# Attention's matmuls in program order, and table products tied behind the softplus split

## The chip, the cores and the metric

The kernel runs on one core of a Trainium2 chip. The metric is device time in microseconds (us) of one execution; the kernel before takes 810.37 us, the median of three runs from 810.09 to 810.9 us.

## The reference, cut to what matters

One decoder layer on a sequence of 512 tokens of width 1024, in float32, with two token mixers side by side:

```
q, k, v, u, g_attn, g_ssm = split(x @ w_in)
A  = stick_breaking_attention(q, k, v) @ w_sb_out      # 8 heads of 64
     # z = q k / 8 ; w = exp(log_sigmoid(z) + sum over later keys of log_sigmoid(-z))
y  = s5_scan(u)                    # 32 groups of 16 channels, 64 complex states each
B  = glu(gelu(y) @ w_glu)
h  = LN1(alpha*x + (sigmoid(g_attn)*A + sigmoid(g_ssm)*B) @ w_o)
h  = LN2(alpha*h + convffn(h) + (p @ w_pe) * sigmoid(h @ w_pe_gate))
```

The S5 scan needs tables that depend on parameters alone (powers of a complex decay, their products with B and C); the kernel computes them on the chip, on DVE.

## The kernel before

Every operand of a matmul is split into a high and a low part (hi is a cast on ACT, lo a subtraction on DVE), and `mm3` makes three matmuls of a product: hi·hi, hi·lo, lo·hi. Weights arrive in pages of 128x1024 by DMA on SP's queue (L102); `split_to` casts them (ACT, L119, `wh`) and subtracts (DVE, L120, `wl`) one page ahead of use.

The stages are: projections u and v; the q/k projections of four pairs of heads; attention beside the projections of pairs 1 to 3 and beside the first of 16 gate projections; the S5 scan beside the other gates; then `mix_attn` (tile A), `mix_ssm` (tile mx), the output projection, the FFN. From the output projection on, nothing is touched by the change.

**Attention** works in 32 units, one for each head h and key block j (3, 2, 1, 0; widths of 128, 256, 384 and 512 queries). Stage a of a unit: three matmuls into z, then Exp and Ln on ACT (tile e), then on DVE a min/max (L210), a cast (L423) and a subtraction (L207) that split the softplus into `sp`. Stage b, five steps later: matmuls of `sp` with a triangle (`tri`) into the same z, two Exp on ACT (w and wp), a subtraction on DVE (wp's low part); the PSUM bank of z comes free here. Stage c, two steps after that: matmuls of wp with v into `av`. The tiles e and w rotate through a pool of six half pages, two or three of which are held by other tiles, so that the Exp of stage b writes to a half page that the softplus split of a recent unit must have left. There are eight PSUM banks for z, av and the projections.

**Order.** The Python program issues the work in an order that generators set: `feature_mms` yields after each third of a projection (8 contraction blocks as 3, 3, 2; called a quantum here), `advance` gives attention 6.5/6 steps for a quantum of q/k and 7/6 for a quantum of a gate, and `interleave` gives the S5 scan 4/3 steps for a quantum of the gates that are left. The S5 steps of a pair of groups pp are `ssm_in` (matmuls V), `ssm_rot`, `ssm_scan` (DVE) and `ssm_out` (matmuls y), with one step of lag from rot to scan and one from scan to out; after the last y a GELU, 16 small DMAs on SP (y<-yst, L828) and a split (yts) lead to the second half of mx. The first half of mx and all of A don't need them.

`Paced` hands out table work: at each step of attention `prep.give(PREP_A)` pays 0.8 us, and the generator `ssm_prep` issues instructions until its declared costs have used that up; what is left is issued after the last step.

The program order is not the order on the engines. The tile framework schedules the whole program by a simulated timeline: an instruction that is ready there may be put ahead of earlier ones on the same engine, and the order on each engine is then fixed. A dependency of the class NoSync between two instructions of one engine fixes their order and adds no semaphore; before, only `actf` uses it, to keep activation tables together.

Of the kernel before, what the change touches and what calls it, by code (L numbers as in the profile page):

```python
# [18 lines left out]
P = 128  # L19
# [150 lines left out]
class Layer:  # L170
# [21 lines left out]


    def mm(self, out, lhsT, rhs, start, stop):
        self.nc.tensor.matmul(out=out, lhsT=lhsT, rhs=rhs, start=start, stop=stop, skip_group_check=True)  # L195

    def mm3(self, out, ah, al, bh, bl, start, stop):
        self.mm(out, ah, bh, start, False)
# [5 lines left out]
        self.nc.vector.tensor_tensor(out=lo, in0=src, in1=hi.bitcast(F32), op=ALU.subtract)  # L204

    def tt(self, out, a, b, op):
        self.nc.vector.tensor_tensor(out=out, in0=a, in1=b, op=op)  # L207

    def stt(self, out, a, s, b, op0, op1):
        self.nc.vector.scalar_tensor_tensor(out=out, in0=a, scalar=s, in1=b, op0=op0, op1=op1)  # L210
# [4 lines left out]
    def actf(self, group, *args, **kw):  # L215

        ins = self.nc.scalar.activation(*args, **kw).ins  # L217
        if group != self.act_group:
            self.act_group, self.act_prev, self.act_cur = group, self.act_cur[-6:], []
        for p in self.act_prev:  # L220
            self.tc.add_manual_dep(ins, p.name, mybir.DependencyInfo(mybir.DependencyClass.NoSync,
                                                                     mybir.DependencyReason.DATA),
                                   reason="table order")
        self.act_cur.append(ins)


# [158 lines left out]
    def attention(self):  # L385

        nc = self.nc
        units = [(h, j) for h in range(NH) for j in (3, 2, 1, 0)]
        st = {}
        prep = self.prep  # L390

        def part(kind, h, j):

            key = (kind, h, j | 2 if j % 2 else j)
            if key not in st:
                st[key] = (self.halves.get(f"{kind}{h}_{j}", F32R, (P, 2, T // 2)) if j == 2 else
                           self.pages.get(f"{kind}{h}_{j}", F32R, (P, 2, T)))
            o = P if j == 1 else 0
            return st[key].t[:, :, o:o + T - P * j]

        def z_of(h, j):

            key = ("z", h, j | 2 if j % 2 else j)
            if key not in st:
                st[key] = self.banks.get(f"z{h}_{j}")
            o = P if j == 1 else 0
            return st[key].t[:, o:o + T - P * j]

        def stage_a(h, j):
            n, q0, r = T - P * j, P * j, slice(HD * (h % 2), HD * (h % 2) + HD)  # L410
            q1, q2, ks = self.qk[h // 2]
            z = z_of(h, j)
            self.mm(z, ks.t[:, h % 2, q0:q0 + P], q1.t[:, h % 2, q0:T], j != 1, False)
            self.mm(z, ks.t[:, h % 2, q0:q0 + P], q2.t[:, h % 2, q0:T], False, False)
            self.mm(z[:, 0:P], self.mask[:, 0], self.mask[:, 1], False, False)
            sp = part("sp", h, j)
            ep = self.halves.get(f"e{h}_{j}", F32, (P, T))
            e = ep.t[:, 0:n]
            self.actf(0, e, z, AF.Exp)
            self.actf(0, e, e, AF.Ln, bias=1.0)  # L420

            self.stt(e, e, 44.0, z, ALU.min, ALU.max)
            nc.vector.tensor_copy(sp[:, 0], e)  # L423
            self.tt(sp[:, 1], e, sp[:, 0].bitcast(F32), ALU.subtract)
            ep.free()

        def stage_b(h, j):
            n = T - P * j
            z, sp = z_of(h, j), part("sp", h, j)
            for half in range(2):  # L430
                self.mm(z, self.tri[:, 0], sp[:, half], False, False)
            for jj in range(j + 1, 4):
                spj = part("sp", h, jj)
                for half in range(2):
                    self.mm(z[:, P * (jj - j):n], self.tri[:, 1], spj[:, half], False, jj == 3 and half == 1)
            wp = part("wp", h, j)
            ep = self.halves.get(f"w{h}_{j}", F32, (P, T))
            w = ep.t[:, 0:n]
            self.actf(0, w, z, AF.Exp)
            self.actf(0, wp[:, 0], z, AF.Exp)  # L440
            if j != 3:
                st.pop(("z", h, j | 2 if j % 2 else j)).free()
            self.tt(wp[:, 1], w, wp[:, 0].bitcast(F32), ALU.subtract)
            ep.free()
            if j == 0:
                for key in (3, 2, 0):
                    st.pop(("sp", h, key)).free()

        def stage_c(h, j):

            q0 = P * j
            wp = part("wp", h, j)
            if j == 3:
                st["av", h] = self.banks.get(f"av{h}")
            av = st["av", h]
            vv = self.v[j].t[:, h].rearrange("p a d -> p (a d)")

            for half in range(2):
                self.mm(av.t[:, q0:T], vv, wp[:, half], j == 3 and half == 0, j == 0 and half == 1)
            if j != 3:  # L460
                st.pop(("wp", h, j | 2 if j % 2 else j)).free()
            if j == 0:
                if h % 4 == 0:
                    self.attn.append(self.pages.get(f"attn{h}", F32, (P, 2, T)))
                r, o = (slice(HD * x, HD * x + HD) for x in (h % 2, 1 - h % 2))
                out = self.attn[h // 4].t[r, (h // 2) % 2]
                nc.scalar.copy(out, av.t[o])
                self.tt(out, out, av.t[r], ALU.add)
                av.free()

        for s in range(len(units) + LAG_C):
            prep.give(PREP_A)
            if s == U_AT:
                self.ssm_u(0)
                self.ssm_u(1)
            if s < len(units):
                while units[s][0] // 2 not in self.qk:
                    yield False
                h, j = units[s]
                stage_a(h, j)  # L480
                if j == 0 and h % 2 == 1:
                    for pg in self.qk[h // 2]:
                        pg.free()
            if 0 <= s - LAG_B < len(units):
                stage_b(*units[s - LAG_B])
            if 0 <= s - LAG_C < len(units):
                stage_c(*units[s - LAG_C])
            yield True
        prep.give(math.inf)


# [156 lines left out]
    def cmul_wide(self, src, n, re, im):  # L648

        t1, t2 = (self.pages.get(f"cm{i}", F32, (P, 4, 16, 16)) for i in range(2))  # L650
        for t, v in ((t1, re), (t2, im)):
            self.tt(t.t[:, 0:n], src, v.unsqueeze(1).unsqueeze(3).to_broadcast([P, n, 16, 16]), ALU.mult)
            yield wide(256 * n)
        return t1, t2

    def ssm_prep(self):
# [2 lines left out]
        cb = self.cbp.t.rearrange("p c r k h -> p (c r) k h")  # L659

        t1, t2 = yield from self.cmul_wide(cb[:, 2:4], 2, *self.coef)
        self.tt(cb[:, 2], t1.t[:, 0], t2.t[:, 1], ALU.subtract)
        self.tt(cb[:, 3], t1.t[:, 1], t2.t[:, 0], ALU.add)
        t1.free()
        t2.free()
        for g in range(2):
            r, h = slice(64 * g, 64 * g + 64), slice(16 * g, 16 * g + 16)
            for ri, sign in ((0, 1.0), (1, -1.0)):
                nc.scalar.mul(self.b0.t[r, ri, :, h], cb[r, 2 + ri], sign)

        self.dd = self.cst.tile([32, 16, 32], F32, name="dd")
        self.tt(self.dd, self.ident[0:32, 0:32].unsqueeze(1).to_broadcast([32, 16, 32]),
                self.d32.unsqueeze(2).to_broadcast([32, 16, 32]), ALU.mult)
        yield wide(512) + 2 * wide(256)

        for m in range(1, 5):
# [3 lines left out]
            for dst, at, i in ((ca, m, 0), (ba, 4 - m, 2 - lo)):  # L680
                if dst is ca and m == 4:
                    continue
                for g in range(2):
                    r, h = slice(64 * g, 64 * g + 64), slice(16 * g, 16 * g + 16)
                    self.tt(dst[r, 0, :, at, h], t1.t[r, i], t2.t[r, i + 1], ALU.subtract)
                    self.tt(dst[r, 1, :, at, h], t1.t[r, i + 1], t2.t[r, i], ALU.add)
                    yield 2 * wide(256)
            t1.free()
            t2.free()
# [3 lines left out]
        for q in range(4):  # L693
            for ri in range(2):
# [2 lines left out]
                    nc.tensor.transpose(bank.t[:, k], ba[:, ri, 4 * q + k].rearrange("p j h -> p (j h)"), self.ident)  # L697
                nc.scalar.copy(self.bl[q].t[:, ri], bank.t)
                bank.free()
                yield wide(512)  # L700

        tab = self.tab = self.ssp.tile([P, 2, 16, P], F32, name="tab", tag="ba_tab")
        nc.vector.memset(tab[:, 0, :, 0:1], 1.0)
# [1 line left out]
        for i in range(7):  # L705
            m = 1 << i
            rot = self.rot[i]
            for k0, nk in ((0, 16),) if m < 64 else ((0, 8), (8, 8)):
# [2 lines left out]
                br, bi = (rot[:, c, ks].unsqueeze(1).unsqueeze(3).to_broadcast([P, 2, nk, m]) for c in range(2))  # L711
                old, new = tab[:, :, ks, 0:m], tab[:, :, ks, m:2 * m]
                n = nk * m
                self.tt(tp.t, old, bi, ALU.mult)
                yield wide(2 * n)
                self.tt(new, old, br, ALU.mult)
                yield wide(2 * n)
                self.tt(new[:, 0], new[:, 0], tp.t[:, 1], ALU.subtract)
                self.tt(new[:, 1], new[:, 1], tp.t[:, 0], ALU.add)
                tp.free()  # L720
                yield 2 * wide(n)

# [458 lines left out]

    def run(self):
        self.qk, self.attn, self.u4, self.pair = {}, [], {}, {}
        self.y, self.gate = [], []
        self.act_group, self.act_prev, self.act_cur = 0, [], []
        self.nc.scalar.preload_act_table_set("natural_log_exp_and_others")
# [11 lines left out]
            self.prep.give(PREP_QK)  # L1198
        att = self.attention()
        self.W.fa = 2  # L1200
        for pair in range(1, 4):
            advance(self.proj_qk(pair), att, QK_RATIO)
        gen = self.gates()
        advance(gen, att, G_RATIO, True)
        for pg in self.v:
            pg.free()
        interleave(gen, self.ssm(), SSM_RATIO)
# [12 lines left out]
        self.ffn_down()  # L1220


def advance(main, side, ratio, to_end=False):

    acc = 0.0
    for _ in main:
        acc += ratio
        while acc >= 1.0:
            acc -= 1.0
            r = next(side, None)  # L1230
            if r is None and to_end:
                return
            if r is False:
                acc = 0.0


@with_exitstack
# [99 lines left out]
```

## Time and profile before

| | us |
|---|---|
| median of 3 runs | 810.37 |
| the profiled execution, its own time | 808.88 |
| its span in the trace | 807.2 |
| PE busy (matmuls) | 789.1 (98%) |
| DVE busy | 509.9 (63%) |
| ACT busy | 331.5 (41%) |
| mean granted clock of PE, share of full | 0.991 |

Busy time of PE is the time in which a matmul is in flight; 18 us of the span have none. The clock that the chip grants to PE is a column of the views by stretches: 1.00 is 2.4 GHz, and a stretch at 1.2 GHz only would show 0.50. The profile is of one execution, and its own time is 1.49 us under the median of the runs.

### The profile page before, as it was taken

How to read it: one execution, taken by the hardware profiler on the slowest of the kernel's cores; microseconds unless marked ns; L12 is line 12 of the kernel's file. 1: busy time of each engine (PE TensorE's matmuls, PEld its weight loads, DVE VectorE, ACT ScalarE, POOL GpSimd, SP SyncE). 2: the span in 40 equal slices, each digit the busy share in tenths (PEclk: the TensorE clock that was granted, in tenths of full speed). 3: DMA queues.
4: the chain of work that ended last, by engine and by line, in shares of the span. 5: the costliest groups of instructions: out<-in, count | busy, mean ns of one | idle time of the engine just before them, and what ended most of it. 6: DMA issues, size and time to landing. Idle time of an engine off the chain costs nothing.

```text
span 807.2 us, 9738 instructions
## 1 busy us (share of the span) xinstructions
PE 789.1 (98%) x3716; PEld 660.2 (82%) x3716; DVE 509.9 (63%) x881; ACT 331.5 (41%) x538; POOL 24.4 (3%) x67
## 2 busy tenths in 40 slices
PE   9999889989999999999999999999999999999996
PEld 7888778878888878888888888888888888888885
DVE  6987975678876857847743756555565565422056
ACT  6435666654343544514433543433443444322000
POOL 0000000000000200004300000000000000000000
PEclk9999999989999999999999999999999999999999
DMA  9913221123113565424303232213312127421002
GB/s 319 390 53 88 70 72 33 53 79 112 45 53 105 208 210 172 166 79 152 109 27 122 85 107 75 84 51 105 105 63 94 53 78 261 157 105 52 1 27 78
DMA packets 29870, 86.73 MB, mean 107 GB/s; under 512 B 4224, under 2 KB 8448, under 8 KB 29568
## 3 DMA queue, kind: packets, MB, share of 16 engines
q1 hardware_dynamic: 27952, 80.35, 29.5%
q0 software_dynamic: 1296, 4.72, 1.6%
q10 hardware_dynamic: 576, 1.05, 0.3%
q8 instruction: 29, 0.48, 0.2%
q14 instruction: 17, 0.14, 0.0%
HBM read 79.81 MB, written 3.15 MB: 103 GB/s over the span
## 4 chain that ended last, share of the span: by engine, by line
PE 91%; DMA 3%; DVE 3%; ACT 2%; issue 1%; DVEq 0%; SPq 0%; ACTq 0%
PE up L195 30%; PE d L195 15%; PE g L195 10%; PE o L195 5%; PE pg L195 5%; PE mx L195 4%; PE z L195 3%; PE qb L195 3%; PE u L195 3%; PE kb L195 3%; PE v L195 3%; PE pe L195 1%; DMA y<-yst 1%; PE y L195 1%; PE av L195 1%; DMA wr<-in_w_sb_out_dram 1%
## 5 line engine op out<-in xcount | busy, mean ns | idle before, releaser
L120 DVE TENSOR_TENSOR wl<-wr,wh 128x1024 fp32r<-128x1024 f32 (+1 forms) x129 | 155.2, 1213 | 98.8 <-ACT wh L119 70.4
L195 PE MATMUL up<-hT,wh 128*128 128x512 f32 x704 | 216.6, 389 | 0.0
L119 ACT CAST wh<-wr 128x1024 fp32r<-128x1024 f32 (+1 forms) x129 | 133.5, 1044 | 161.2 <-PE d L195 38.1
L195 PEld LDWEIGHTS up<-hT,wh 128*128 128x128 f32 x704 | 132.1, 188 | 27.3
L195 PE MATMUL up<-hT,wl 128*128 128x512 f32 x352 | 136.9, 389 | 0.0
L195 PE MATMUL d<-wh,act 128*128 128x512 f32 (+1 forms) x364 | 109.1, 382 | 0.0
L210 DVE SCALAR_TENSOR_TENSOR cv<-up,cw,cv 128x511 f32<-128x511 f32 x88 | 65.8, 747 | 32.4 <-ACT cv L1120 30.9
L195 PE MATMUL g<-xs,wh 128*128 128x512 f32 x256 | 81.5, 398 | 0.0
L195 PEld LDWEIGHTS d<-wh,act 128*128 128x128 f32 x364 | 67.6, 188 | 13.2
L195 PEld LDWEIGHTS up<-hT,wl 128*128 128x128 f32 x352 | 66.1, 188 | 13.8
L195 PE MATMUL d<-wl,act 128*128 128x512 f32 (+1 forms) x182 | 69.5, 382 | 0.0
L1120 ACT ACTIVATE cv<-up,cb,cw 128x512 f32<-128x512 f32 x44 | 34.2, 777 | 59.0 <-PE up L195 59.0
L195 PEld LDWEIGHTS g<-xs,wh 128*128 128x128 f32 x256 | 46.5, 189 | 9.0 <-issue 0.6
L195 PE MATMUL g<-xs,wl 128*128 128x512 f32 x128 | 49.9, 391 | 0.0
L195 PE MATMUL pg<-wh,hT 128*128 128x512 f32 x128 | 40.1, 390 | 0.0
L195 PE MATMUL o<-wh,mx 128*128 128x512 f32 x128 | 40.1, 391 | 0.0
L195 PEld LDWEIGHTS d<-wl,act 128*128 128x128 f32 x182 | 34.2, 188 | 6.7
L195 PE MATMUL mx<-yts,wh 128*128 128x512 f32 x128 | 39.6, 389 | 0.0
L195 PE MATMUL z<-sp,tri 128*128 128x128 f32 (+3 forms) x160 | 30.5, 324 | 5.0 <-DVE e L210 2.1
L195 PEld LDWEIGHTS z<-sp,tri 128*128 128x128 f32 x160 | 27.4, 209 | 8.0 <-DVE sp L207 2.7
L207 DVE TENSOR_TENSOR cv<-cv 128x512 f32<-128x512 f32 x22 | 15.2, 692 | 24.5 <-ACT cv L217 24.5
L207 DVE TENSOR_TENSOR x<-x,d 128x512 f32<-128x512 f32 (+1 forms) x10 | 6.1, 606 | 35.1 <-PE d L195 35.1
(180 smaller groups left out, 1142.4 us busy)
## 6 DMA issues: line engine op xcount, KB each, us to landing
wr<-in_w_up_dram SPq DMA_DIRECT2D x44, 512.0 KB, 3.3
wr<-in_w_down_dram SPq DMA_DIRECT2D x22, 512.0 KB, 3.3
wr<-in_w_g_dram SPq DMA_DIRECT2D x16, 512.0 KB, 3.3
wr<-in_w_qk_dram SPq DMA_DIRECT2D x8, 512.0 KB, 11.7
wr<-in_w_glu_dram SPq DMA_DIRECT2D x8, 512.0 KB, 3.8
wr<-in_w_o_dram SPq DMA_DIRECT2D x8, 512.0 KB, 4.1
wr<-in_w_pe_gate_dram SPq DMA_DIRECT2D x8, 512.0 KB, 3.3
wr<-in_w_uv_dram SPq DMA_DIRECT2D x7, 512.0 KB, 7.6
```

The source lines that it names most:

```text
L119: self.nc.scalar.copy(hi.t[:, c], raw.t[:, c])
L120: self.nc.vector.tensor_tensor(out=lo.t[:, c], in0=raw.t[:, c], in1=hi.t[:, c].bitcast(F32), op=ALU.subtract)
L195: self.nc.tensor.matmul(out=out, lhsT=lhsT, rhs=rhs, start=start, stop=stop, skip_group_check=True)
L207: self.nc.vector.tensor_tensor(out=out, in0=a, in1=b, op=op)
L210: self.nc.vector.scalar_tensor_tensor(out=out, in0=a, scalar=s, in1=b, op0=op0, op1=op1)
L1120: nc.scalar.activation(y, bank.t, AF.Identity, scale=cw[:, 2:3], bias=cb)
```

## The change

The matmuls from the projection of pair 1 to the end of attention are chained in program order by NoSync dependencies. Each wide table product and sum on DVE is chained behind the last softplus split issued before it. `advance` starts the first of its calls with minus one step, so attention's first unit is issued one quantum later. The seven last steps of attention, which have no stage a, count as 1.8 steps, so more gate quanta are issued beside them. The declared cost of a transposition of the table `ba` falls from wide(512), 0.69, to 0.3, so that more table work is issued for the same pay. No instruction is added or removed.

```diff
     def mm(self, out, lhsT, rhs, start, stop):
-        self.nc.tensor.matmul(out=out, lhsT=lhsT, rhs=rhs, start=start, stop=stop, skip_group_check=True)
+        ins = self.nc.tensor.matmul(out=out, lhsT=lhsT, rhs=rhs, start=start, stop=stop, skip_group_check=True).ins
+        if self.in_order:
+            if self.last_mm is not None:
+                self.after(ins, self.last_mm)
+            self.last_mm = ins
+
+    def after(self, ins, prev):
+        self.tc.add_manual_dep(ins, prev.name, mybir.DependencyInfo(mybir.DependencyClass.NoSync,
+                                                                    mybir.DependencyReason.DATA), reason="order")
+    def tt_wide(self, out, a, b, op):
+        ins = self.tt(out, a, b, op)
+        if self.last_sp is not None:
+            self.after(ins, self.last_sp)
...
-            self.tt(sp[:, 1], e, sp[:, 0].bitcast(F32), ALU.subtract)
+            self.last_sp = self.tt(sp[:, 1], e, sp[:, 0].bitcast(F32), ALU.subtract)
...
                 while units[s][0] // 2 not in self.qk:
-                    yield False
+                    yield 0.0
...
-            yield True
+            yield 1.0 if s < len(units) else 1.8
...
-            self.tt(t.t[:, 0:n], src, v.unsqueeze(1).unsqueeze(3).to_broadcast([P, n, 16, 16]), ALU.mult)
+            self.tt_wide(t.t[:, 0:n], src, v.unsqueeze(1).unsqueeze(3).to_broadcast([P, n, 16, 16]), ALU.mult)
...
                 nc.scalar.copy(self.bl[q].t[:, ri], bank.t)
                 bank.free()
-                yield wide(512)
+                yield 0.3
...
         self.W.fa = 2
+        self.in_order = True
         for pair in range(1, 4):
-            advance(self.proj_qk(pair), att, QK_RATIO)
+            advance(self.proj_qk(pair), att, QK_RATIO, start=-1.0 if pair == 1 else 0.0)
         gen = self.gates()
         advance(gen, att, G_RATIO, True)
+        self.in_order = False
...
-def advance(main, side, ratio, to_end=False):
-    acc = 0.0
+def advance(main, side, ratio, to_end=False, start=0.0):
+    acc = start
     for _ in main:
         acc += ratio
         while acc >= 1.0:
-            acc -= 1.0
             r = next(side, None)
             if r is None and to_end:
                 return
-            if r is False:
-                acc = 0.0
+            acc = acc - (r or 1.0) if r != 0.0 else 0.0
```

The other calls of `self.tt` in `cmul_wide` and `ssm_prep` (tiles cm, cb, dd, ca, ba, tabtmp, tab) become `self.tt_wide` in the same way.

## Rows read from the trace of the kernel before

**Rows 1.** Busy time by engine in stretches from attention to the end of A

```profile
core 0: us, PE busy (x) PEld busy (x) DVE busy (x) ACT busy (x) POOL busy (x), PEclk, DMA share, GB/s
64.00:124.00 60.00, 54.40 (x286) 46.89 (x285) 50.07 (x103) 36.04 (x82) 0.00 (x0) 0.97 0.25 74
124.00:176.00 52.00, 49.28 (x267) 42.89 (x267) 32.13 (x79) 34.86 (x77) 0.00 (x0) 0.93 0.19 61
...
199.00:279.00 80.00, 80.00 (x454) 68.67 (x453) 63.01 (x105) 33.84 (x61) 2.02 (x10) 1.00 0.31 98
279.00:304.00 25.00, 24.40 (x108) 19.86 (x107) 13.10 (x18) 13.57 (x15) 2.95 (x6) 1.00 0.63 218
```

**Rows 2.** The same view, the stretches of 4 us around the two largest stalls

```profile
116.00:120.00 4.00, 1.82 (x10) 1.16 (x8) 3.89 (x11) 1.60 (x3) 0.00 (x0) 1.00 0.38 87
120.00:124.00 4.00, 3.27 (x11) 2.98 (x12) 3.91 (x9) 2.29 (x6) 0.00 (x0) 0.58 0.20 46
164.00:168.00 4.00, 1.67 (x12) 1.38 (x10) 3.90 (x16) 2.69 (x7) 0.00 (x0) 1.00 0.41 133
168.00:172.00 4.00, 3.64 (x12) 2.95 (x13) 2.88 (x7) 2.58 (x6) 0.00 (x0) 0.56 0.67 200
172.00:176.00 4.00, 4.00 (x18) 3.61 (x18) 2.61 (x7) 3.62 (x9) 0.00 (x0) 0.59 0.21 60
```

**Rows 3.** Waits from 64 to 199 us: total, times, longest in us

```profile
ACT w L217 <- DVE sp L207: 15.8, 9, 4.4
...
PE z L195 <- DVE e L210: 2.7, 2, 2.1
...
PE z L195 <- DVE sp L207: 2.0, 1, 2.0
...
PE qb L195 <- ACT wp L217: 1.1, 1, 1.1
```

**Rows 4.** Timeline of DVE at the first large stall: start, us, instruction

```profile
118.06 1.18 DVE L207 TENSOR_TENSOR ba<-cm,cm 64x256 f32<-64x256 f32 x3
...
119.53 0.42 DVE L207 TENSOR_TENSOR ba<-cm,cm 64x256 f32<-64x256 f32 x1
119.98 0.69 DVE L207 TENSOR_TENSOR sp<-e,sp 128x512 fp32r<-128x512 f32 x1
```

**Rows 5.** Timeline of PE behind that split, idle time before it in brackets

```profile
120.73 2.18 PE L195 MATMUL z<-sp,tri 128*128 128x512 f32 x7 [2.04 <-DVE sp L207]
```

**Rows 6.** Timeline of DVE before attention's first unit

```profile
56.77 1.53 DVE L207 TENSOR_TENSOR ca<-cm,cm 64x256 f32<-64x256 f32 x4
58.31 1.53 DVE L207 TENSOR_TENSOR ba<-cm,cm 64x256 f32<-64x256 f32 x4
```

**Rows 7.** Chain of waits: the projection behind q of pair 0

```profile
60.43 5.44 PE kb L195 x24
```

**Rows 8.** Timeline of SP: the DMAs of q, pair 0

```profile
61.08 2.53 SPq L380 DMA_DIRECT2D q<-q  x4
```

**Rows 9.** View of tile q from 50 to 75 us: issue to landing

```profile
DMA to landing us min/median/max: 2.2/2.3/3.1
```

**Rows 10.** Matmuls grouped by line, 199 to 271 us: the gates

```profile
L195 PE MATMUL g<-xs,wh 128*128 128x512 f32 x144 | 46.0, 401 | 0.0
L195 PE MATMUL g<-xs,wl 128*128 128x512 f32 x72 | 28.1, 390 | 0.0
```

**Rows 11.** Timeline of PE: last V, and mx's second half

```profile
261.80 1.05 PE L195 MATMUL V<-u,bl 128*128 128x128 f32 x8
...
270.86 0.62 PE L195 MATMUL A<-ats,wh 128*128 128x512 f32 x2
...
303.05 0.84 PE L195 MATMUL mx<-yts,wh 128*128 128x512 f32 x3
```

**Rows 12.** DVE grouped by line, 262.8 to 276.5 us: what is not the scan

```profile
L120 DVE TENSOR_TENSOR wl<-wr,wh 128x1024 fp32r<-128x1024 f32 x3 | 3.7, 1218 | 0.2 <-ACT wh L119 0.2
L207 DVE TENSOR_TENSOR yts<-y,yts 128x512 fp32r<-128x512 f32 x2 | 2.2, 1090 | 0.0
```

More of the change, by code (lines that the diff above doesn't have):

```diff
@@ L206, in tt @@
     def tt(self, out, a, b, op):
-        self.nc.vector.tensor_tensor(out=out, in0=a, in1=b, op=op)
+        return self.nc.vector.tensor_tensor(out=out, in0=a, in1=b, op=op).ins
+    def tt_wide(self, out, a, b, op):
+        ins = self.tt(out, a, b, op)
+        if self.last_sp is not None:
+            self.after(ins, self.last_sp)
     def stt(self, out, a, s, b, op0, op1):
@@ L220, in actf @@
         for p in self.act_prev:
-            self.tc.add_manual_dep(ins, p.name, mybir.DependencyInfo(mybir.DependencyClass.NoSync,
-                                                                     mybir.DependencyReason.DATA),
-                                   reason="table order")
+            self.after(ins, p)
         self.act_cur.append(ins)
@@ L661, in ssm_prep @@
         t1, t2 = yield from self.cmul_wide(cb[:, 2:4], 2, *self.coef)
-        self.tt(cb[:, 2], t1.t[:, 0], t2.t[:, 1], ALU.subtract)
-        self.tt(cb[:, 3], t1.t[:, 1], t2.t[:, 0], ALU.add)
+        self.tt_wide(cb[:, 2], t1.t[:, 0], t2.t[:, 1], ALU.subtract)
+        self.tt_wide(cb[:, 3], t1.t[:, 1], t2.t[:, 0], ALU.add)
         t1.free()
@@ L671, in ssm_prep @@
         self.dd = self.cst.tile([32, 16, 32], F32, name="dd")
-        self.tt(self.dd, self.ident[0:32, 0:32].unsqueeze(1).to_broadcast([32, 16, 32]),
+        self.tt_wide(self.dd, self.ident[0:32, 0:32].unsqueeze(1).to_broadcast([32, 16, 32]),
                 self.d32.unsqueeze(2).to_broadcast([32, 16, 32]), ALU.mult)
@@ L684, in ssm_prep @@
                     r, h = slice(64 * g, 64 * g + 64), slice(16 * g, 16 * g + 16)
-                    self.tt(dst[r, 0, :, at, h], t1.t[r, i], t2.t[r, i + 1], ALU.subtract)
-                    self.tt(dst[r, 1, :, at, h], t1.t[r, i + 1], t2.t[r, i], ALU.add)
+                    self.tt_wide(dst[r, 0, :, at, h], t1.t[r, i], t2.t[r, i + 1], ALU.subtract)
+                    self.tt_wide(dst[r, 1, :, at, h], t1.t[r, i + 1], t2.t[r, i], ALU.add)
                     yield 2 * wide(256)
@@ L713, in ssm_prep @@
                 n = nk * m
-                self.tt(tp.t, old, bi, ALU.mult)
+                self.tt_wide(tp.t, old, bi, ALU.mult)
                 yield wide(2 * n)
-                self.tt(new, old, br, ALU.mult)
+                self.tt_wide(new, old, br, ALU.mult)
                 yield wide(2 * n)
-                self.tt(new[:, 0], new[:, 0], tp.t[:, 1], ALU.subtract)
-                self.tt(new[:, 1], new[:, 1], tp.t[:, 0], ALU.add)
+                self.tt_wide(new[:, 0], new[:, 0], tp.t[:, 1], ALU.subtract)
+                self.tt_wide(new[:, 1], new[:, 1], tp.t[:, 0], ALU.add)
                 tp.free()
@@ L1183, in run @@
         self.qk, self.attn, self.u4, self.pair = {}, [], {}, {}
+        self.in_order, self.last_mm, self.last_sp = False, None, None
         self.y, self.gate = [], []
```

## The prediction, made before the change was run

> **What bounds the kernel now.** I read the busy times by stretches first, to see where PE, which is busy for 98% of the span, is not. In the scan's stage, between 199 and 279 us, PE has no idle time at all [rows 1]; a change of order can win nothing there and can only lose. Attention is the place: PE is idle for 60.00 - 54.40 = 5.60 us between 64 and 124 us and for 52.00 - 49.28 = 2.72 us between 124 and 176 us, 8.32 us together [rows 1]. Then I cut these stretches into pieces of 4 us, to see what follows an idle time. Behind the two largest ones (2.18 us of 116 to 120, 2.33 us of 164 to 168) the mean granted clock falls to 0.58, 0.56 and 0.59, a mix of the 2.4 and the 1.2 GHz level; at these means the three pieces lose 4 x (0.42 + 0.44 + 0.41) = 5.1 us of matmul time [rows 2]. So attention's stalls cost at most 8.3 + 5.1 = 13.4 us. "At most", since idle time inside a slow piece is counted twice.
>
> What ends the stalls is in the waits: of PE's own, 4.7 us are for DVE's min/max and softplus split, and the largest wait of all is ACT's, 15.8 us for the split, because the Exp of stage b writes to a half page that the split must have left [rows 3]. DVE is not idle then: in both pieces with a stall it is busy for 3.89 and 3.90 of 4 us [rows 2]. The timeline shows with what. Four sums of the table ba stand directly ahead of the subtraction of a split [rows 4], and PE, which has its triangle matmuls next, stands still for 2.04 us [rows 5]. The scheduler put those matmuls there for a simulated DVE that was earlier than the real one.
>
> **The change, part by part.** Nothing is added to any engine: no matmul, product or DMA more, and the chains are between instructions of one engine, so no semaphore. All terms are order.
>
> *The table tie* takes the cause of the large stalls away: a product may not pass the split issued before it. It is a wait for DVE too: a tied product whose split is late holds up the weight splits (wl) and wp subtractions queued behind it, for which the gates and av wait. It forbids what the kernel does now at 56.77 us, where eight table sums, 1.53 + 1.53 us, fill DVE before the first unit exists [rows 6]; by the pay, three of the four pairs of sums belong to attention's first steps, 2.3 us that move into the fullest stretch. There DVE was busy for 50.07 us [rows 1]; with 2.3 more it needs 52.4 us, and PE without its stalls would want 60 - 5.6 - 1.7 = 52.7 us. At the 3.9 of 4 us that DVE reaches at its fullest [rows 2], 52.4 us of work take 53.7 us. So DVE gives back 1 us if its waits are hidden, and all 5.6 us of idle time there if it does no better than the 83% of before; I take 2 us, nearer to its fullest pieces, since they show that it can.
>
> *The matmul chain.* In program order stage b follows stage a by five steps, with 6 quanta beside 6.5 units. A quantum is a third of 5.44 us [rows 7], so five steps hold some 8 us of projections and the units' own matmuls, against a softplus chain of five instructions, none longer than the widest subtraction's 0.69 us [rows 4], so at most 3.5 us if nothing is ahead of them (an estimate). That margin is what the scheduler's order spent. The price is that whatever is late holds the whole queue. Writing the order down by hand, I count 12 places where a PSUM bank is asked for 1.4 to 2.8 us of matmuls after the work that frees it (two Exp on ACT, or the copy of av). Today such a wait costs PE 1.1 us, once [rows 3]. The bounds are 0 and 12 x 1.1 = 13 us; I take 3 us, a quarter of a microsecond each, because ACT is busy for only 36 of 60 us there [rows 1] and most of these distances are above 2 us.
>
> *The first unit* comes after two quanta instead of one. q ends at 60.43 us, where the next projection begins [rows 7]; its four DMAs are issued in 2.53 us from 61.08 us on [rows 8], and land 2.2 to 3.1 us later [rows 9]. The first two, which unit 0 needs, land at about 64.1 us. Two quanta of 3/8 x 5.44 = 2.04 us each put its matmuls at 64.5 us. No stall; one quantum earlier it would be 62.5 us, and 1.6 us lost under the chain. Cost nothing, with 0.4 us of cover; uncovered, at most the 3.1 - 2.2 = 0.9 us by which a landing varies [rows 9].
>
> *More gates beside the last units.* With 5 + 6 + 6 units beside q/k instead of 18, and seven last steps at 1.8, attention takes 15 + 12.6 = 27.6 credits and ends in the 25th gate quantum; before, 21 credits and the 19th. So 23 quanta, not 29, are left beside the scan. On the chip the difference is smaller: the trace has 216 gate matmuls from 199 us on, 27 quanta [rows 10], so two had been pulled forward. Their weight DMAs move along on SP, past the loads of u; at a DMA share of 0.19 to 0.25 [rows 1] I charge nothing, and if that cover went, a page's landing would show as PE waiting for wl. PE's work is the same in sum. What it uncovers is the end of the scan. Of the scan's 36 steps 30 are now issued beside gates, so the last V comes behind the last gate. Now V starts at 261.80 us and the second half of mx, which needs the y after it, at 303.05 us [rows 11]: 41.2 us that PE fills, but for 0.60 us idle [rows 1], with y, A, the first half of mx, and, between V and A's start at 270.86 us [rows 11], 6.8 us of gates (30 matmuls at 5.44/24). If V goes behind the gates, those 6.8 us are missing. The hole is 0 if the scheduler pulls V forward as it does now, or if DVE drops other work from the way: three wl and two yts, 3.7 + 2.2 us [rows 12], stand between V and y. I take 2.5 us: those splits belong to A and mx and only some can go elsewhere.
>
> *The cheaper transpositions* issue table work earlier: 8 x 0.39 = 3.1 us of pay, four steps. It uses DVE's idle time of 124 to 176 us (52 - 32.13 = 19.9 us [rows 1]). Nothing, unless the gates beside it lose their wl.
>
> **Sum.** -13.4 + 2 + 3 + 2.5 = -5.9 us. On the profiled execution, 808.88 us, that is 803.0 us; the median of the runs stands 1.49 us above it, so I forecast 804.5 us.
>
> **Rivals.** *All of it.* DVE keeps up, ACT frees the banks in time, V is pulled forward; only 1 us stays: -12.4 us, 798.0 us. For it speaks that each stall of more than 2 us has table work in it; against it, that DVE needs 99% of the q/k stretch. Chance 0.15.
>
> *The buffers, not the order.* If all 12 bank places cost the 1.1 us that one costs now, 13.2 us come back and the time is 810.2 us, no change. For it: the 15.8 us of ACT are a wait for a half page [rows 3]. Against it: the table sums in the middle of a split are an order, and they are untied from no buffer. Chance 0.12. The Trainium skill, Perfetto Trace Analysis, Optimization Strategy, says that the same gap repeating on the engine that should be saturated can mean that SBUF or PSUM lacks room for the next tile; by that rule order would change little here. The trace agrees for ACT's wait and not for PE's two long stalls, which are of different lengths, 48 us apart.
>
> *Slower: the end of the scan.* The hole takes its full 6.8 us, and a hole of that kind is followed by a slow clock as in attention (up to 4 x (0.44 + 0.41) = 3.4 us [rows 2]): 10.2 us against a gain of 13.4 - 2 - 3 = 8.4 us, +1.8 us, 812.2 us. It decides where the hole exceeds what attention wins, and with DVE at its other bound (5.6 for 2) it is +5.4 us. For it: PE is full there and mx waits for 16 DMAs that nothing shortens. Against it: A can start earlier, and the scheduler is not chained in that stage. Chance 0.17. That the chain changes nothing is excluded: the trace has triangle matmuls ahead of older work.
>
> **How the numbers follow.** The forecast has 0.56, the rivals 0.15, 0.12 and 0.17. About 0.2%, 1.6 us, is what a measurement of this kernel can tell from no change. Faster holds the forecast less 0.01 and the first rival, 0.70; same 0.13; slower 0.17. The range runs from just under the first rival, 797.5 us, to the slower one, 812.5 us; beyond it lie DVE's worst bound with a full hole and a gain without any remainder. The forecast's own range is 800 to 808.5 us.
>
> **What would show it.** Right: between 64 and 176 us of work PE idles for 2 to 6 us, the clock stays at 1.00, no table product stands inside a split, and ACT's wait for sp falls well under 15.8 us; gates from 199 us on fall to about 23 quanta; the stall before mx's second half grows to some 3 us. Wrong: many PE waits of about 1 us for wp or attn (the buffers), a wait of 5 us or more for yts or a slow clock near 280 us (the scan's end), or DVE over 97% busy with PE waiting for sp throughout.

## The result, and the profile after

The changed kernel takes 802.47 us, the median of five runs from 802.31 to 803.08 us, against 810.9 us for the kernel before beside it: a ratio of 0.990, with a 95% interval from 0.9885 to 0.9914. The profiled execution is the run of 802.31 us, with a span of 800.6 us; it stands 0.16 us under its median. The forecast was 804.5 us.

The busy times by stretch, as in [rows 1] (PE, PEld, DVE, ACT, POOL, granted clock, DMA share, GB/s):

```profile
64.00:124.00 60.00, 58.10 (x308) 49.34 (x307) 54.99 (x116) 39.99 (x88) 0.00 (x0) 1.00 0.28 82
124.00:176.00 52.00, 48.47 (x277) 42.05 (x277) 39.73 (x91) 34.22 (x75) 0.00 (x0) 1.00 0.16 52
...
199.00:271.00 72.00, 72.00 (x410) 61.39 (x410) 52.94 (x92) 30.07 (x55) 0.74 (x7) 1.00 0.27 88
271.00:300.00 29.00, 27.63 (x133) 22.79 (x133) 20.02 (x29) 15.56 (x17) 3.95 (x8) 1.00 0.60 200
```

PE's idle time in attention fell less than one might think, from 5.60 + 2.72 = 8.32 us to 1.90 + 3.53 = 5.43 us, and in the second stretch it even rose. The clock column is what changed wholly: 0.97 and 0.93 became 1.00 and 1.00. The same view in the pieces of 4 us that hold the three largest stalls answers to [rows 2]:

```profile
108.00:112.00 4.00, 3.18 (x19) 2.71 (x18) 3.91 (x9) 2.81 (x7) 0.00 (x0) 1.00 0.00 0
136.00:140.00 4.00, 2.51 (x17) 2.15 (x17) 2.74 (x6) 3.97 (x9) 0.00 (x0) 1.00 0.00 0
164.00:168.00 4.00, 2.37 (x14) 1.81 (x13) 3.94 (x9) 1.96 (x5) 0.00 (x0) 1.00 0.00 0
```

The pieces lack 0.82, 1.49 and 1.63 us of PE, where before they lacked 2.18 and 2.33 us, and no piece from 60 to 200 us is below 1.00 in the clock. So the chip kept 2.4 GHz throughout attention. The waits of 64 to 199 us, as in [rows 3]:

```profile
ACT w L232 <- DVE sp L216: 4.5, 4, 1.5
...
PE z L195 <- ACT wp L232: 2.0, 3, 1.6
...
PE bt L710 <- ACT wp L232: 1.0, 1, 1.0
PE av L195 <- ACT wp L232: 0.8, 1, 0.8
...
PE z L195 <- DVE e L225: 0.6, 1, 0.6
PE z L195 <- DVE attn L216: 0.6, 1, 0.6
...
PE av L195 <- DVE attn L216: 0.3, 1, 0.3
```

ACT's wait for the half page that a split must leave went from 15.8 to 4.5 us, and PE no longer waits for a split (sp) at all. Of what is left, 3.8 us are for the Exp that frees a PSUM bank or fills wp, and 1.5 us for DVE's min/max (e) and its sum of attention's outputs (attn).

At the end of the scan, PE's timeline, which answers to [rows 11]:

```profile
261.09 1.06 PE L195 MATMUL V<-u,bl 128*128 128x128 f32 x8
261.90 0.71 PE L195 MATMUL A<-ats,wh 128*128 128x512 f32 x2
...
297.08 1.66 PE L195 MATMUL mx<-yts,wh 128*128 128x512 f32 x6 [1.37 <-DVE yts L903]
```

The last V stands behind the last gate now, with A directly after it, and the second half of mx waits 1.37 us; before, 0.60 us of the same stretch was idle. And the gates from 199 us on, as in [rows 10]:

```profile
L195 PE MATMUL g<-xs,wh 128*128 128x512 f32 x118 | 37.9, 402 | 0.0
L195 PE MATMUL g<-xs,wl 128*128 128x512 f32 x60 | 23.4, 390 | 0.0
```

That is 178 matmuls or 22 quanta, against 27.

The account of the profiled executions: idle time of attention -2.9 us, slow clock -5.1 us, the end of the scan +0.8 us, -7.2 us in all, where their own times differ by 802.31 - 808.88 = -6.6 us. So attention gave back 8.0 us.

### The profile page after: what moved, and what is told of

It is laid out like the page before. It is cut to its first block, busy times and chain, and to the rows that moved or that the text cites. A ratio compares the mean times of both kernels' runs of the same rounds, so it can differ in the third digit from the quotient of the medians.

```text
span 800.6 us, 9760 instructions
## 1 busy us (share of the span) xinstructions
PE 784.6 (98%) x3716; PEld 655.8 (82%) x3716; DVE 508.2 (63%) x881; ACT 333.1 (42%) x538; POOL 24.2 (3%) x67
## 4 chain that ended last, share of the span: by engine, by line
PE 92%; DVE 3%; ACT 2%; DMA 2%; issue 1%; SPq 1%; DVEq 0%; ACTq 0%
PE up L195 30%; PE d L195 15%; PE g L195 10%; PE o L195 5%; PE pg L195 5%; PE mx L195 4%; PE z L195 3%; PE u L195 3%; PE v L195 3%; PE kb L195 2%; PE qb L195 2%; PE A L195 2%; PE pe L195 1%; PE y L195 1%; DMA y<-yst 1%; PE av L195 1%
## 5 line engine op out<-in xcount | busy, mean ns | idle before, releaser
L195 PEld LDWEIGHTS mx<-yts,wh 128*128 128x128 f32 x128 | 24.0, 188 | 6.7 <-DVE yts L903 1.8
L195 PEld LDWEIGHTS g<-xs,wl 128*128 128x128 f32 x128 | 24.0, 188 | 5.2
```

Source lines behind the costliest of these rows:

```text
L195: ins = self.nc.tensor.matmul(out=out, lhsT=lhsT, rhs=rhs, start=start, stop=stop, skip_group_check=True).ins
```

## The experiments

All runs below are of five rounds beside the kernel before, whose medians were 810.28, 810.18 and 810.57 us in the three groups, and 810.9 us beside the changed kernel; times are medians. Between groups the same kernel thus moved by 0.7 us, so a difference of less than 1 us between groups is not shown by the times alone. The diffs of the first six (down to 36/23 scan steps in the table) are against the changed kernel. For each I also read two numbers from its trace, both from 60 to 200 us: PE's idle time, and the clock loss, the sum over pieces of 4 us of 4 x (1 - mean granted clock). They are of the one profiled execution. A piece without a matmul counts too, so that 1.2 us of the 5.1 us of "no tie" cost no matmul time.

| kernel | us | PE idle, 60 to 200 | clock loss |
|---|---|---|---|
| before | 810.2 to 810.9 | 8.3 | 5.1 |
| changed | 802.47 | 5.4 | 0.0 |
| changed, no chain | 804.5 | 2.6 | 3.4 |
| changed, no tie | 814.32 | 14.0 | 5.1 |
| changed, first unit early | 803.99 | 4.7 | 0.0 |
| changed, tail at 1.0 | 801.7 | 5.4 | 0.0 |
| changed, old pay | 801.73 | 3.9 | 0.0 |
| changed, 36/23 scan steps | 801.47 | 5.4 | 0.0 |
| chain alone | 810.85 | 11.0 | 5.1 |
| tie alone | 809.98 | 7.9 | 6.9 |
| tie and tail | 812.52 | 7.9 | 6.9 |
| tie and first unit | 802.58 | 4.7 | 5.1 |
| chain and tie | 801.28 | 5.1 | 0.0 |
| chain, tie and first unit | 799.73 | 3.8 | 0.0 |

Three of these executions lose clock once more, outside the columns: "no chain", "first unit early" and "tie and tail" lose some 1.7 us each behind PE's wait for yts near 300 us.

**One part taken back: the chain.**

```diff
-        self.in_order = True
+        self.in_order = False
```

> The changed kernel without the matmul chain (in_order stays False); tie, first unit, tail of 1.8 and cheap transpositions stay. Theory 'the chain': the scheduler's own order of matmuls is what stands PE still, so most of the 8.4 us go back: 808 to 812 us, with stalls of 2 us and more in attention and a granted clock under 0.95 behind them. Rival 'the table tie': the products inside the split were the cause, the chain adds nothing: 801 to 804 us, clock 1.00.

804.5 us, from 802.41 to 806.40 us in two groups of three; ratio to before 0.9926 (0.9905 to 0.9948). So the chain is worth some 2 us in this company, and not most of the gain. That it is worth anything here is not clear of noise: the intervals of the two ratios overlap (from 0.9905 here, up to 0.9914 for the changed kernel), and three of the six runs, up to 802.94 us, are as quick as the changed kernel's. The profiled run, of 806.4 us, has less idle time in attention than the changed kernel, but a stall that the clock follows. Busy times of three pieces:

```profile
104.00:108.00 4.00, 2.33 (x9) 1.79 (x8) 3.94 (x8) 2.24 (x5) 0.00 (x0) 0.72 0.21 79
108.00:112.00 4.00, 3.73 (x11) 2.98 (x11) 3.91 (x9) 3.52 (x7) 0.00 (x0) 0.50 0.00 0
112.00:116.00 4.00, 4.00 (x20) 3.44 (x20) 3.96 (x10) 0.52 (x3) 0.00 (x0) 0.93 0.00 0
...
300.00:304.00 4.00, 4.00 (x12) 3.08 (x12) 4.00 (x6) 1.05 (x1) 0.00 (x0) 0.57 0.13 52
```

PE lacks 1.67 us in the first piece, after which a whole piece runs at 0.50: 1.2 GHz. But attention is the smaller part of it: its span is 4.1 us longer than the changed kernel's (804.7 for 800.6 us), and attention makes 0.6 us of that, 2.8 us less idle time against 3.4 us of slow clock. The rest stands at the start, where PE waits 1.6 us for the first split of x, and at the end of the scan, where it waits 2.00 us for yts instead of 1.37 and the clock then falls, as the last line shows (4 x 0.43 = 1.7 us).

**The tie.**

```diff
         ins = self.tt(out, a, b, op)
-        if self.last_sp is not None:
-            self.after(ins, self.last_sp)
```

> The changed kernel without the tie of the wide table products; the chain stays. Theory 'the chain': little is lost, 802 to 805 us, PE idle in attention of 5 to 8 us in pieces under 2 us. Rival 'the table tie': 807 to 811 us, since products again run ahead of the splits and the chained PE waits for them.

814.32 us, 4 us over the kernel before (ratio 1.005, 1.0033 to 1.0068): more than either expected, 11.9 us for the one part. The timelines of three engines show the whole mechanism in one place. DVE first:

```profile
171.37 0.35 DVE L434 CAST sp<-e 128x384 fp32r<-128x384 f32 x1
171.75 0.42 DVE L223 SCALAR_TENSOR_TENSOR e<-e,z 128x256 f32<-128x256 f32 x1
172.09 2.35 DVE L216 TENSOR_TENSOR tab<-tab,pair_buf 128x1024 f32<-128x1024 f32 x2
174.36 0.55 DVE L216 TENSOR_TENSOR sp<-e,sp 128x384 fp32r<-128x384 f32 x1
174.83 0.29 DVE L434 CAST sp<-e 128x256 fp32r<-128x256 f32 x1
175.15 0.42 DVE L216 TENSOR_TENSOR sp<-e,sp 128x256 fp32r<-128x256 f32 x1
```

Two products of the table, 2.35 us, sit between the cast and the subtraction of a split (128x384). The next split (128x256), whose min/max is done before them, comes behind both. ACT wants the half page of this second split for w:

```profile
175.61 0.38 ACT L230 ACTIVATE w<-z 128x256 f32<-128x256 f32 x1 [6.01 <-DVE sp L216]
```

And PE, which wants the PSUM bank that this Exp and the one after it free, and, being chained, does nothing else meanwhile:

```profile
176.32 1.22 PE L195 MATMUL z<-q,ks 128*128 128x512 f32 x2 [7.63 <-ACT wp L230]
```

**The first unit.**

```diff
-            advance(self.proj_qk(pair), att, QK_RATIO, start=-1.0 if pair == 1 else 0.0)
+            advance(self.proj_qk(pair), att, QK_RATIO, start=0.0)
```

> The changed kernel with the first unit one quantum earlier (start 0). By the timing of q's DMAs (landing at about 64.1 us, matmuls wanted at 62.5 us) the chained PE waits 1.6 us at the first unit: 803.5 to 805 us, with one idle piece near 62 to 64 us. Rival: the wait is made up later, since attention as a whole has slack at its tail: 802 to 803 us.

803.99 us, from 803.14 to 804.34, so 1.5 us slower. PE's waits show the wait for q that the expectation put at 1.6 us, and a longer one at the end of the scan:

```profile
PE mx L195 <- DVE yts L903: 2.2, 1, 2.2
...
PE z L195 <- DMA q<-q: 1.4, 2, 1.0
```

The wait for q isn't where the time went, though. In attention as a whole PE idles less than in the changed kernel, 4.7 us for 5.4, so the early wait is made up within attention, as the rival expected. What is longer is the wait for yts, 2.16 us for 1.37, and the clock falls behind it, for 0.9 + 0.8 = 1.7 us:

```profile
296.00:300.00 4.00, 2.68 (x8) 2.17 (x9) 3.36 (x5) 1.05 (x1) 0.00 (x0) 0.78 0.38 132
300.00:304.00 4.00, 4.00 (x15) 3.21 (x15) 3.12 (x4) 0.00 (x0) 0.00 (x0) 0.80 0.17 60
```

So 1.5 us agrees with 1.6 us by luck. A cleaner pair stands further down: with chain and tie alone, the early unit costs 801.28 - 799.73 = 1.55 us in one group, and 5.1 - 3.8 = 1.3 us of idle time in attention.

**The tail, and the pay of the transpositions.**

```diff
-            yield 1.0 if s < len(units) else 1.8
+            yield 1.0
```

> The changed kernel with the last seven steps at 1.0 instead of 1.8: 19 gate quanta beside attention, 29 beside the scan. Theory: in the tail of attention each step then has less beside it and the chained PE waits for Exp and av, 2 to 4 us of idle time, while the stall ahead of mx's second half goes from 1.4 us to under 0.7 us: 803 to 806 us. Rival 'the end of the scan': the tail costs nothing, and the missing hole makes it faster: 801 to 802 us.

801.7 us, from 801.40 to 802.03, below every run of the changed kernel, though by the ratios (0.9893 for 0.990, intervals overlapping) the difference is not shown. Idle time in attention is the same 5.4 us, so the fuller tail covers nothing; and from 271 to 300 us PE is busy without a break:

```profile
271.00:300.00 29.00, 29.00 (x135) 24.24 (x134) 15.43 (x20) 16.13 (x18) 3.83 (x7) 1.00 0.72 241
```

```diff
-                yield 0.3
+                yield wide(512)
```

> The changed kernel with the transpositions at the old pay of 0.69 us. Theory: that part only moves table work into DVE's idle time; within 1 us of the changed kernel, 801.5 to 803.5 us. Rival: the table work left for the end of attention delays the scan's first products and with them the scan, 804 to 806 us.

801.73 us, from 801.03 to 803.91, which overlaps the changed kernel's runs: no difference that five runs can tell. The trace does show one, in both directions: PE idles 3.9 us in attention instead of 5.4, where the wait of the transpositions (bt, which are not in the chain), 1.0 us, has almost gone, and waits 1.97 us for yts instead of 1.37.

**The end of the scan.**

```diff
-SSM_RATIO = 4 / 3
+SSM_RATIO = 36 / 23
```

> The changed kernel with 36/23 scan steps for a gate quantum instead of 4/3, so that all 36 steps of the scan lie beside the 23 quanta that are left. If the stall of 1.4 us ahead of mx's second half comes from the last V standing behind the last gate, V moves some 8 us ahead of it and the stall goes: 800.5 to 801.8 us. Rival: DVE sets the pace of the scan, so V moves but y does not, or PE now waits inside the scan: 802 to 805 us.

801.47 us, from 800.42 to 802.65. PE no longer waits for yts, and the last V moved from 261.09 us to

```profile
257.67 1.05 PE L195 MATMUL V<-u,bl 128*128 128x128 f32 x8
```

That is 5.7 us ahead of A's first matmul, where some 8 us were expected. With the tail at 1.0 the same wait went by the other way, with more gates left behind V. Both agree that it comes from V's place behind the gates. By the trace it is worth 1.37 us; the times are 1.0 and 0.8 us lower, which alone would not show it.

**One part alone.** These are the kernel before with one part of the change, written as the changed kernel without the others (first unit, tail and pay as before):

```diff
-        if self.last_sp is not None:
-            self.after(ins, self.last_sp)
...
-            advance(self.proj_qk(pair), att, QK_RATIO, start=-1.0 if pair == 1 else 0.0)
+            advance(self.proj_qk(pair), att, QK_RATIO, start=0.0)
...
-            yield 1.0 if s < len(units) else 1.8
+            yield 1.0
...
-                yield 0.3
+                yield wide(512)
```

> The kernel before with the matmul chain alone: no tie, first unit as before, tail at 1.0, transpositions at full pay. Theory 'the chain': it carries more than half of the gain alone, 803 to 807 us, PE's clock at 1.00 in attention. Rival 'only together': the chain alone makes PE wait for splits behind table products and for q at the first unit: 808 to 814 us.

810.85 us (ratio 0.9995, 0.9983 to 1.0008): no change. Eight table sums stand between the cast and the subtraction of one split, and PE's longest wait is behind it. DVE's timeline, then PE's:

```profile
88.90 0.42 DVE L434 CAST sp<-e 128x512 fp32r<-128x512 f32 x1
89.23 1.52 DVE L216 TENSOR_TENSOR ca<-cm,cm 64x256 f32<-64x256 f32 x4
90.77 1.53 DVE L216 TENSOR_TENSOR ba<-cm,cm 64x256 f32<-64x256 f32 x4
92.32 0.23 DVE L434 CAST sp<-e 128x128 fp32r<-128x128 f32 x1
92.47 0.69 DVE L216 TENSOR_TENSOR sp<-e,sp 128x512 fp32r<-128x512 f32 x1
```

```profile
94.38 0.80 PE L195 MATMUL z<-q,ks 128*128 128x256 f32 x2 [5.30 <-ACT wp L230]
```

The tie alone has `in_order = False` in place of the first two lines of that diff.

> The kernel before with the table tie alone. Theory 'the chain': 808 to 812 us, the long stalls stay with other releasers than table products. Rival 'the table tie': 802 to 806 us, the two stalls of over 2 us gone and the clock at 1.00.

809.98 us (ratio 0.9994, 0.9984 to 1.0004): no change either. Stalls stay, and the longest one has no table product in it now. PE's timeline, then DVE's, then ACT's:

```profile
98.20 0.69 PE L195 MATMUL z<-q,ks 128*128 128x128 f32 x2 [2.87 <-ACT wp L232]
```

```profile
94.56 0.36 DVE L436 CAST sp<-e 128x384 fp32r<-128x384 f32 x1
94.83 1.22 DVE L120 TENSOR_TENSOR wl<-wr,wh 128x1024 fp32r<-128x1024 f32 x1
96.08 0.69 DVE L225 SCALAR_TENSOR_TENSOR e<-e,z 128x512 f32<-128x512 f32 x1
96.69 0.55 DVE L216 TENSOR_TENSOR sp<-e,sp 128x384 fp32r<-128x384 f32 x1
```

```profile
95.69 1.03 ACT L119 CAST wh<-wr 128x1024 fp32r<-128x1024 f32 x1
97.27 0.49 ACT L232 ACTIVATE w<-z 128x384 f32<-128x384 f32 x1 [0.55 <-DVE sp L216]
```

A weight split and another unit's min/max stand in the split's way, both things that the tie doesn't order. ACT's own queue takes part: a weight cast stands ahead of w, which then waits only 0.55 us for the split. In total ACT's wait for sp fell from 15.8 only to 11.5 us.

**Pairs and the best of the parts.** `chain and tie` is the diff above without its first two lines; the run after it also keeps `start=-1.0`.

> The kernel before with chain and tie and nothing else (first unit early, tail at 1.0, transpositions at full pay). Each alone moved nothing, and taking the first unit, the tail and the pay back one by one moved +1.5, -0.8 and -0.7 us. Theory 'chain and tie need each other': both together carry the whole gain, 801.5 to 803.5 us. Rival 'all five parts': without the first unit's delay and the fuller tail half of the gain is gone, 805 to 808 us.

801.28 us, from 800.69 to 802.28 (ratio 0.989, 0.9867 to 0.9912). Two parts that move nothing alone carry, together, all of the change's gain. They are not the only pair that does, as the last run shows.

> Chain, tie and the later first unit; tail at 1.0 and full pay as in the kernel before. Theory: the two parts left out only cost the stall ahead of mx's second half, so this is the fastest of all, 800 to 801.7 us, with no wait of PE for yts. Rival: the single removals don't add, 802 to 803 us.

799.73 us, from 798.95 to 799.85 (ratio 0.9868, 0.9844 to 0.9892): the fastest of all, below every run of the changed kernel, and under the expectation. PE waits in attention for 3.8 us and not at all for yts. The tail and the pay, of which each cost some 0.8 us or less when taken back by itself, cost 802.47 - 799.73 = 2.7 us together. The traces say why the single removals show less: the tail brings the wait for yts and the pay the idle time in attention, 1.4 and 1.6 us in this pair, but with the old pay alone the wait for yts grows.

The last two have no chain (`in_order = False`), the old pay, and one of the first unit and the tail.

> No chain: tie and tail of 1.8 only. The tie alone gave 809.98 us, the changed kernel without the chain 804.5 us, so of first unit, tail and pay something gives 5.5 us there. Theory 'more to fill with': the free scheduler uses the gates that the tail sets free, 804 to 807 us. Rival 'the first unit': 808.5 to 811 us.

812.52 us (ratio 1.0016, 1.0001 to 1.0032). Idle time and clock loss of attention are those of the tie alone, and PE waits 2.5 us more for yts, with a clock loss behind it, so the theory of more gates to fill with falls.

> No chain: tie and later first unit only. Theory 'more to fill with' (the tail): 808 to 811 us. Rival 'the first unit': it spares the scheduler an early cluster of units, 803 to 806 us. If this and the run with the tail both lie near 810 us, the 5.5 us come from the pay of the transpositions or from a single stall that another order happens to miss.

802.58 us, from 801.40 to 804.64 (ratio 0.9905, 0.9878 to 0.9931). The rival holds: one unit later, the free scheduler stumbles less, 4.7 us of idle time for 7.9. In the profiled run, one of 804.4 us, the clock still falls. Why one unit less has that effect without the chain wasn't tried further.

So the tie has two partners. With the later first unit and no chain it gains as much as the whole change (0.9905 for 0.990); with the chain and no later first unit too (0.989); with neither it gains nothing (809.98 and 812.52 us). With both it gains most: the chain then adds 802.58 - 799.73 = 2.9 us, in one group and with no run in common, and the clock loss goes from 5.1 us to none. No kernel without the tie gained. The later first unit was not run alone.

## Why the prediction was right

The time, 802.47 us, lies in the range and 2.0 us under the forecast. Of the 2.0 us, 1.3 come from the step from a profiled execution to the median, put at 1.49 us and here 0.16 us; for the profiled execution itself 803.0 us were forecast and 802.31 measured. The sum was right with its main terms: 8.4 us forecast for attention and 8.0 us won, a hole of 2.5 us and 0.8 us. What it says of the single parts was not. By its steps:

**The stalls and the clock, 13.4 us at most.** Right. The table shows no clock loss in attention in any kernel with both chain and tie, and 3.4 to 6.9 us in every one without one of them. The clock was the larger part of attention's gain: 5.1 us of 8.0.

**What stays in attention, 2 us for DVE and 3 us for the banks.** 5.4 us stayed. The waits for Exp, 2.0 + 1.0 + 0.8 us, are the banks and wp; the other 1.5 us are e and attn, DVE. Of the 12 places five became waits, and these cost more than the quarter of a microsecond each that the prediction took: 0.8 us on average, up to 1.6 us. DVE did get full, 27.43 of 28 us:

```profile
76.00:104.00 28.00, 27.15 (x149) 23.25 (x149) 27.43 (x57) 18.11 (x42) 0.00 (x0) 1.00 0.25 64
```

PE lost only 0.85 us there, so the slack of five steps held in that stretch.

**The first unit, nothing with it and 1.6 us without.** Half right. The wait for q's DMAs was there, 1.4 us, but in the run that took this part out of the change the 1.5 us of time stand at the end of the scan, and the two figures agree by luck. And "cost nothing" missed what the later unit is worth: without the chain it alone decides whether the tie gains.

**More gates, a hole of 2.5 us.** The order was right (22 quanta left, V behind the last gate), the size was not: the hole grew by 0.8 us. The step that failed is the 41.2 us from V to the second half of mx. That was when PE came to it, behind matmuls of A, and not when it could have begun. DVE's casts of the last y, before and then after, tell:

```profile
298.22 1.09 DVE L890 CAST yts<-y 128x512 fp32r<-128x512 f32 x2
```

```profile
296.40 1.08 DVE L903 CAST yts<-y 128x512 fp32r<-128x512 f32 x2 [2.63 <-DMA y<-yst]
```

From V to these casts it is 36.4 us before and 35.3 us after: a chain that hardly changed, with some 4 us of cover more than the prediction gave it. As a part of the change the tail is a loss all the same: it brings the wait of 1.37 us and saves no idle time in attention.

**The cheaper transpositions, nothing.** Wrong by the traces: PE's idle time in attention is 5.4 us with them and 3.9 us at the old pay. In time, alone, nothing that can be told; together with the tail they cost 2.7 us.

**What was wrong** is that the prediction gave tie and chain a term each, the tie "takes the cause of the large stalls away" and the chain gives margin. Neither does anything alone. What the runs show in its place is that the tie works in company, of the chain or of the later first unit, and the chain only beside the tie. And "no table product stands inside a split" is not so in the changed kernel: the tie holds a product behind the split issued before it, not out of the next one. In DVE's timeline two products stand between the cast and the subtraction of the split 128x384:

```profile
108.46 0.36 DVE L436 CAST sp<-e 128x384 fp32r<-128x384 f32 x1
108.74 0.42 DVE L216 TENSOR_TENSOR sp<-e,sp 128x256 fp32r<-128x256 f32 x1
109.07 0.75 DVE L216 TENSOR_TENSOR ca<-cm,cm 64x256 f32<-64x256 f32 x2
109.74 0.54 DVE L216 TENSOR_TENSOR sp<-e,sp 128x384 fp32r<-128x384 f32 x1
```

The rivals: *the buffers* would have left 810.2 us. Without one buffer more, ACT's wait for a half page fell to 4.5 us. The sentence of the Trainium skill, Perfetto Trace Analysis, Optimization Strategy, that a repeated gap can mean a lack of SBUF or PSUM, fits part of what is left, 2.0 + 1.0 us of PE's waits for a bank, and not what went. *The end of the scan* has the place right and a price of 0.8 us for 6.8; the slow clock behind the hole, which it feared, did not come in the changed kernel (1.00 from 271 to 300 us) but did in three of the variants, behind waits of 2.0 to 2.5 us. *All of it* was out by the 5.4 us that stay, though leaving out two parts comes within 1.7 us of its 798.0 us.

## What to carry to other kernels

Where a scheduler orders engines by a simulated time, ask which of its orders the chip cannot keep. An order fixed on one engine only moves the wait to the next: here the chain alone and the tie alone each measured as nothing, and the tie gained once PE's order was fixed too or the first unit came later. So a part that "does nothing" in a trial by itself may be half of a gain. Count the clock with the stalls: here, spreading idle time into pieces that the clock did not follow was worth more (5.1 us) than removing some of it (2.9 us). Take a change apart after it has won, since two of its five parts were costing 2.7 us. And when a variant is slower by about the expected amount, look over its whole span for the time: the early first unit lost 1.4 us where it was expected to, won it back, and was slower by a wait and a slow clock more than 200 us later.

## What was not expected of the hardware

The same length of stall was followed by 1.2 GHz in one place and not in another. One stall of 1.67 us was in the kernel without the chain (the pieces from 104 us above), and not in the kernel without the tie, whose stall of 1.67 us ends at 95.50 us:

```profile
92.00:96.00 4.00, 2.33 (x11) 1.63 (x10) 3.91 (x10) 1.82 (x4) 0.00 (x0) 1.00 0.43 98
96.00:100.00 4.00, 4.00 (x25) 3.55 (x24) 3.86 (x9) 1.75 (x4) 0.00 (x0) 1.00 0.10 22
```

In the changed kernel stalls of 1.49 and 1.63 us in a piece were not. Ahead of mx's second half a wait of 1.97 us (old pay) was not, and one of 2.00 us (no chain) was. So the length of a stall alone doesn't tell; what does wasn't tried.

The runs of the kernel without the chain lie in two groups 3.6 us apart. That the same program sometimes keeps the clock over a stall would explain it, and the mean granted clock that is on record for every run speaks for it: 0.994 in the three runs near 802.6 us, 0.990 to 0.992 in the three near 806.2 us. That is 1.6 to 3.2 us of 803 us, half of the gap or more. At which stall the clock differs isn't shown, since only one of the runs has a profile.
